# A hybrid decoder layer on one core: the state-space loop as small steps in one written order

## The chip, the core and the metric

One core of a Trainium2 chip runs the whole layer in one launch. Times are microseconds (us) on the device; the time of a kernel is the median of its runs. TensorE is called PE in the profile (PEld for its weight loads), VectorE DVE, ScalarE ACT, GpSimd POOL, and SyncE, which here only issues DMAs, SP. The profile comes from one further execution.

## What is computed

`x` is (1, 2048, 1024) float32. One layer:

```python
h = rmsnorm(x, pre_norm_g)
u_s, z_s, q, k, v, z_a, g_s, g_a = split(h @ w_in)              # 8192 columns
y_s = s5_branch(u_s, ...) * silu(z_s)
y_a = dilated_attention_branch(q, k, v) * silu(z_a)
merged = sigmoid(g_s) * (y_s @ w_branch_s) + sigmoid(g_a) * (y_a @ w_branch_a)
x = x + rmsnorm(merged @ w_out, post_norm_g)
```

The s5 branch has 32 groups of 16 channels, each with 64 complex states that decay along the sequence:

```python
lam_bar = exp(lam * dt);  b_bar = ((lam_bar - 1) / lam) * b
drive  = einsum('gpc,blgc->blgp', b_bar, ug)
states = associative_scan(a_r * a_l, a_r * b_l + b_r)(lam_bar, drive)
y = gelu(einsum('gcp,blgp->blgc', c, states).real + d_skip * u)
y = y * sigmoid(y @ w_glu + b_glu)
```

## The kernel before

`h` stays in SBUF as two float32r halves, `hhi` and `hlo`, and every product of it with a weight is made of three matmuls (high by high, high by low, low by high). A strip of `w_in` is 128 columns. A **bank** is one PSUM tile of 128x512 that PE fills: 24 matmuls of 512 columns for the strips of the gates (`proj`, L103) or 48 matmuls of 256 columns for the values (`values`, L118). Between the first projections and the attention there are 96 banks: 32 for the gate `g_s` (evicted by a tanh on ACT, L559), 16 for `z_s` (tanh on ACT, then one operation on DVE, `ze`, L571 and L572) and 48 for the values (a copy on ACT, `ve`, L121). Each evicted bank goes to DRAM by a DMA. `feed` (L577) hands the banks out one by one and loads the next pair of strips, four transfers `w_raw` and four splits `w_hi` (ACT, L43) and `w_lo` (DVE, L44), when a pair is used up.

In between the banks runs the state-space loop: 16 passes, each over a **pair** of groups. For a pair,

- `ssm_powers` makes the tables `q` and `out` on POOL;
- `ssm_setup` makes on PE a small kernel `pk` (L444) and a transpose `pt` (L458), evicts them (`kt` on DVE, L446; `inm` on ACT, L460), and writes `kt` to DRAM and reads it back as the Toeplitz matrix `toep`;
- `ssm_states` makes the rotations `rot_c` (POOL) and `rot_s` (DVE, L485 to L487), the drive `pd` on PE (L499, needs `inm`), its copy on ACT (L501), and then swaps halves of the partitions by two DMAs (L493, L494), rotates (POOL L506, DVE L505 and L507), scans (DVE L510), swaps again, and rotates back (POOL L516, DVE L515 and L519) into `st`;
- `ssm_outputs` makes `py` on PE (L529, L530, needs `st` and `toep`) and a gelu of it: a square on ACT (L537), two operations on DVE (L538, L539), a tanh on ACT (L540), one on DVE (L541), two DMAs.

What is in order: on PE the order is written by hand. `queued` (L594) ties each piece of PE work to the one before it, so in `run` a pass is `pd`, two banks, `py` of the pair before, a bank, `pk` and `pt` of the next pair, a bank. On the other engines and on the DMA queue of SP the order inside a pass is the scheduler's: the kernel is built with `schedule_with_timeline_sim=True`, and the scheduler sorts what is ready by its own estimate of time. Once built, each engine takes its instructions in the order in which they stand, and one that waits holds those behind it. After the loop come `glu`, the remaining banks, the attention (`unit`), its combination, the branch products and the output.

Of the kernel before, what the change touches and what calls it, by code (L numbers as in the profile page):

```python
# [34 lines left out]
class Builder:  # L35
    def __init__(self, tc, a):
        self.tc, self.nc, self.a = tc, tc.nc, a

# [54 lines left out]

    def proj(self, ps, w, s, chunk):
# [12 lines left out]
    def values(self, ev, psum, w, g, p):  # L107

        nc = self.nc
        hi, lo = w  # L110
        for r in range(0, 16, 2):
            ps = psum.tile([128, 2, 256], F32, tag="proj", name="pv")
            for o in range(2):
                rs = slice((r + o) * 128, (r + o) * 128 + 128)
                n = 0
                for k in range(8):
                    for st, m in ((self.hhi, hi), (self.hhi, lo), (self.hlo, hi)):
                        last = nc.tensor.matmul(ps[:, o], st[:, k, rs], m[:, k], start=n == 0, stop=n == 23)  # L118
                        n += 1
            e = ev.tile([128, 2, 256], F32, tag="ev", name="ve")  # L120
            nc.scalar.activation(e, ps, AF.Copy)  # L121
            cols = slice(256 * p, 256 * p + 256)
            if g == 0:
                dst = self.vd[0].rearrange("(i r) x -> i r x", r=16)[:, r : r + 2, cols]
            elif g == 1:
                m, c = divmod(r, 4)
                dst = self.vd[1].rearrange("(c i m) x -> m i c x", c=4, m=4)[m][:, c : c + 2, cols]
            else:
                dst = self.vd[2].rearrange("(r i) x -> i r x", r=16)[:, r : r + 2, cols]
            nc.sync.dma_start(dst, e)  # L130
            yield last
# [276 lines left out]
    def ssm_powers(self, g0, pool, tabd):  # L408

        nc = self.nc  # L410
        MUL, SUB = ALU.mult, ALU.subtract
        tab = pool.tile([128, 2, TAB], F32, name="tab", bufs=3)
        nc.sync.dma_start(tab, tabd[:, g0 : g0 + 2])
        sh = [128, 2, 16, 8]

        def power(which, n0):
            o = TABS[which][0] + n0
            return tab[:, :, o : o + 8].unsqueeze(2).to_broadcast(sh)

        def wide(which):  # L420
            o = TABS[which][0]
            return tab[:, :, o : o + 16].unsqueeze(3).to_broadcast(sh)

        g = nc.gpsimd
        t8 = pool.tile(sh, F32, name="t8")
        q = pool.tile(sh, F32, name="q", bufs=2)
        out = pool.tile(sh, F32, name="out", bufs=3)
        g.tensor_tensor(q, wide(6), power(4, 0), op=MUL)
        g.tensor_tensor(t8, wide(7), power(5, 0), op=MUL)
        g.tensor_tensor(q, q, t8, op=SUB)  # L430
        ot, t8t = (x.rearrange("p g c t -> p g (c t)").rearrange("p g (t c) -> p g c t", t=8) for x in (out, t8))
        g.tensor_tensor(ot, wide(8), power(4, 1), op=MUL)
        g.tensor_tensor(t8t, wide(9), power(5, 1), op=MUL)
        g.tensor_tensor(ot, ot, t8t, op=SUB)
        return tab, q, out

    def ssm_setup(self, g0, powers, pool, psum, kds):
        nc = self.nc
        tab, q, out = powers
        cs, dg = (tab[:, :, TABS[i][0] : TABS[i][0] + 16] for i in (8, 10))  # L440

        pk = psum.tile([128, 2, 16], F32, tag="s", name="pk")
        for j in range(2):
            nc.tensor.matmul(pk[:, j], q[:, j].rearrange("p c t -> p (c t)"), cs[:, j], start=True, stop=True)  # L444
        kt = pool.tile([128, 2, 16], F32, name="kt")
        nc.vector.tensor_tensor(kt, pk, dg, op=ALU.add)  # L446


        kd = kds[g0 // 2 % 2]
        toep = pool.tile([128, 2, 128], F32, name="toep", bufs=2)  # L450
        for j in range(2):
            nc.sync.dma_start(kd[j, :, 7:], kt[:, j])
            windows = bass.AP(tensor=kd.tensor, offset=kd[j].offset, ap=[[15 * 16, 16], [16, 8], [1, 128]])
            nc.sync.dma_start(toep[:, j], windows)

        pt = psum.tile([128, 2, 128], F32, tag="t", name="pt")
        for j in range(2):
            last = nc.tensor.transpose(pt[:, j], q[:, j].rearrange("p c t -> p (c t)"), self.ident)  # L458
        inm = pool.tile([128, 2, 128], F32, name="inm", bufs=2)
        nc.scalar.activation(inm, pt, AF.Copy)  # L460
        return last, (tab, inm, toep, out)

    def ssm_input(self, g0, pool):
        u = pool.tile([128, 2, 256], F32, name="u", bufs=2)
        ud = self.ud.rearrange("ch s k i -> (ch s) (k i)")
        self.nc.sync.dma_start(u, ud[g0 * 128 : g0 * 128 + 256].rearrange("(g p) x -> p g x", p=128))
        return u

    def ssm_states(self, g0, u, mats, pool, psum):

        nc = self.nc
        MUL, ADD, SUB = ALU.mult, ALU.add, ALU.subtract
        tab, inm, toep, out = mats

        sh = [128, 2, 16, 16]
        ca, sa = (tab[:, :, TABS[i][0] : TABS[i][0] + 16].unsqueeze(3).to_broadcast(sh) for i in (0, 1))
        cb, sb = (tab[:, :, TABS[i][0] : TABS[i][0] + 16].unsqueeze(2).to_broadcast(sh) for i in (2, 3))
        c, s = (pool.tile(sh, F32, name=n) for n in ("rot_c", "rot_s"))
        t = pool.tile(sh, F32, tag="sx", name="rot_t", bufs=SXB)
        w = pool.tile(sh, F32, tag="sx", name="rot_w", bufs=SXB)  # L480
        g = nc.gpsimd
        g.tensor_tensor(c, ca, cb, op=MUL)
        g.tensor_tensor(t, sa, sb, op=MUL)
        g.tensor_tensor(c, c, t, op=SUB)
        nc.vector.tensor_tensor(s, sa, cb, op=MUL)  # L485
        nc.vector.tensor_tensor(w, ca, sb, op=MUL)
        nc.vector.tensor_tensor(s, s, w, op=ADD)  # L487
        c = c.rearrange("p g a b -> p g (a b)")
        s = s.rearrange("p g a b -> p g (a b)")

        def swapped(x):
            y = pool.tile([128, 2, 256], F32, tag="sx", name="sx", bufs=SXB)
# [4 lines left out]
        pd = psum.tile([128, 2, 256], F32, tag="s", name="pd")  # L497
        for j in range(2):
# [79 lines left out]
    def feed(self, wp, items):  # L578
# [11 lines left out]
        while ready:  # L590
            yield from ready.pop(0)
            prepare()
# [582 lines left out]
```

## Time and profile before

| | |
|---|---|
| median of 3 runs | 2167.76 us (2166.22 to 2170.51) |
| the profiled execution's own time | 2165.64 us |
| its span, first to last instruction | 2163.8 us |
| PE busy | 2091.1 us, 97% of the span, 11668 matmuls |
| PEld, DVE, ACT, POOL busy | 83%, 42%, 27%, 18% |
| mean granted clock of TensorE | 0.988 |
| the loop, first `pd` (pair 0) to first `pd` of pair 15 | 231.40 to 665.34 us |

A timeline row gives start, duration, engine, line, operation, result and operands, and in square brackets how long the engine was idle before it and what ended that. Matmuls are pipelined, so a matmul's duration is longer than the distance to the next one's start; lengths of PE's work are therefore read from start to start.

### The profile page before, as it was taken

Reading aid. Unit: us, or ns where it says so; the run is one execution under the profiler, and the core shown is the slowest. Engines: PE = TensorE matmul, PEld = TensorE weight load, DVE = VectorE, ACT = ScalarE, POOL = GpSimd, SP = SyncE. Lnnn points to the kernel's source line nnn. Section 1 sums busy time; section 2 is a strip of 40 time slices with the busy share of each in tenths; the row PEclk is TensorE's granted clock in tenths of the full one; section 3 lists DMA queues with packets and bytes.
Section 4 is the critical chain, followed back from the end, with each engine's and each line's share of the span. In section 5 each row is a group of like instructions: output and inputs, shape, how many; then the busy total and the mean of one; then the engine's idle time right before and its main releaser. Section 6 shows DMA issues by size and latency. Waiting matters only on the chain.

```text
span 2163.8 us, 30793 instructions
## 1 busy us (share of the span) xinstructions
PE 2091.1 (97%) x11668; PEld 1799.8 (83%) x11668; DVE 915.1 (42%) x2261; ACT 587.6 (27%) x1327; POOL 388.1 (18%) x384
## 2 busy tenths in 40 slices
PE   8999999999989999999999999999899999999998
PEld 6788877798889997888888888888677878999987
DVE  6981345544443223423433442442512125544435
ACT  5421111111112323333433432443111124211211
POOL 0002344443331120000000000000555301111111
PEclk9999999999999999999999999999999999999999
DMA  7243233333333551111111111121666437343423
GB/s 251 90 149 131 84 102 99 92 96 109 106 93 113 167 153 45 43 60 58 59 50 59 60 50 59 54 64 54 185 214 188 144 117 224 104 147 107 122 78 98
DMA packets 208373, 231.50 MB, mean 107 GB/s; under 512 B 24864, under 2 KB 142944, under 8 KB 207968
## 3 DMA queue, kind: packets, MB, share of 16 engines
q1 hardware_dynamic: 208224, 229.54, 34.2%
q8 instruction: 91, 1.49, 0.3%
q14 instruction: 58, 0.48, 0.1%
HBM read 146.52 MB, written 74.56 MB: 102 GB/s over the span
## 4 chain that ended last, share of the span: by engine, by line
PE 67%; DMA 13%; DVE 9%; issue 3%; POOL 3%; SPq 2%; ACT 2%; DVEq 0%; POOLq 0%; ACTq 0%
PE proj L103 40%; PE br L937 7%; PE po L956 7%; DMA sx<-sx 3%; PE pv L118 3%; DMA cf<-fd 2%; PE s L762 2%; DMA w_raw<-in_wst_dram 2%; PE glu L634 1%; DMA kd<-kt 1%; PE nb L788 1%; DVE rot_s L485 1%; DMA raw<-in_wout_dram 1%; DVE sx L507 1%; POOL sx L506 1%
## 5 line engine op out<-in xcount | busy, mean ns | idle before, releaser
L103 PE MATMUL proj<-hhi,w_hi 128*128 128x512 f32 x1664 | 672.6, 405 | 27.9 <-DVE ze L572 12.5
L103 PE MATMUL proj<-hlo,w_hi 128*128 128x512 f32 x1664 | 667.4, 401 | 3.4 <-DVE hlo L44 2.7
L103 PE MATMUL proj<-hhi,w_lo 128*128 128x512 f32 x1664 | 666.2, 401 | 0.0
L103 PEld LDWEIGHTS proj<-hhi,w_hi 128*128 128x128 f32 x1664 | 315.6, 190 | 107.1 <-DVE ze L572 15.2
L103 PEld LDWEIGHTS proj<-hlo,w_hi 128*128 128x128 f32 x1664 | 315.6, 190 | 78.3 <-DVE hlo L50 3.5
L103 PEld LDWEIGHTS proj<-hhi,w_lo 128*128 128x128 f32 x1664 | 315.9, 190 | 71.8
L118 PE MATMUL pv<-w_hi,hhi 128*128 128x256 f32 x768 | 223.1, 291 | 4.5 <-ACT ve L121 2.7
L118 PE MATMUL pv<-w_lo,hhi 128*128 128x256 f32 x768 | 217.6, 283 | 0.0
L118 PE MATMUL pv<-w_hi,hlo 128*128 128x256 f32 x768 | 217.5, 283 | 0.0
L44 DVE TENSOR_TENSOR w_lo<-w_raw,w_hi 128x512 fp32r<-128x512 f32 (+1 forms) x130 | 93.1, 735 | 263.2 <-ACT w_hi L43 262.7
L118 PEld LDWEIGHTS pv<-w_hi,hhi 128*128 128x128 f32 x768 | 148.1, 193 | 6.2 <-ACT ve L121 3.3
L118 PEld LDWEIGHTS pv<-w_lo,hhi 128*128 128x128 f32 x768 | 148.0, 193 | 0.8
L118 PEld LDWEIGHTS pv<-w_hi,hlo 128*128 128x128 f32 x768 | 147.7, 192 | 0.0
L746 ACT ACTIVATE p<-p,nm 128x256 f32<-128x256 f32 (+1 forms) x192 | 89.5, 467 | 162.2 <-DVE nm L745 146.1
L740 DVE CUSTOM_DVE_ANT_0 p<-s,mask 128x256 f32<-128x256 f32 (+1 forms) x192 | 68.1, 375 | 144.9 <-PE t L821 69.6
L43 ACT ACTIVATE w_hi<-w_raw 128x512 fp32r<-128x512 f32 (+1 forms) x130 | 77.8, 620 | 180.3 <-DMA w_raw<-in_wst_dram 136.8
L940 POOL TENSOR_TENSOR gt<-gt 128x256 f32<-128x256 f32 x64 | 48.7, 764 | 388.7 <-DVE gt L939 226.2
L956 PE MATMUL po<-wout0h,mh 128*128 128x512 f32 x256 | 99.0, 392 | 2.1 <-ACT wout0h L43 2.1
L696 POOL CAST kh<-kh 128x128 fp32r<-128x128 f32 x12 | 4.0, 334 | 538.5 <-PE s L818 429.7
L956 PE MATMUL po<-wout0l,mh 128*128 128x512 f32 x256 | 99.9, 390 | 0.0
L956 PE MATMUL po<-wout0h,ml 128*128 128x512 f32 x256 | 99.5, 390 | 0.0
L559 ACT ACTIVATE ge<-proj 128x512 f32<-128x512 f32 x64 | 37.7, 592 | 180.0 <-PE proj L103 110.0
(249 smaller groups left out, 3369.8 us busy)
## 6 DMA issues: line engine op xcount, KB each, us to landing
w_raw<-in_wst_dram SPq DMA_DIRECT2D x126, 256.0 KB
vd<-ve SPq DMA_DIRECT2D x48, 256.0 KB
numd<-acc SPq DMA_DIRECT2D x48, 256.0 KB
cn<-numd SPq DMA_DIRECT2D x48, 256.0 KB
cf<-fd SPq DMA_DIRECT2D x48, 256.0 KB
xT<-in_xT_dram SPq DMA_DIRECT2D x32, 256.0 KB
gts<-ge SPq DMA_DIRECT2D x32, 256.0 KB
sx<-sx SPq DMA_DIRECT2D x64, 128.0 KB
```

The source lines that it names most:

```text
L43: nc.scalar.activation(hi, src, AF.Copy)
L44: nc.vector.tensor_tensor(lo, src, raw(hi), op=ALU.subtract)
L103: last = nc.tensor.matmul(ps, st[:, k, cs], m, start=n == 0, stop=n == 23)
L118: last = nc.tensor.matmul(ps[:, o], st[:, k, rs], m[:, k], start=n == 0, stop=n == 23)
L485: nc.vector.tensor_tensor(s, sa, cb, op=MUL)
L559: nc.scalar.activation(e, ps, AF.Tanh, scale=0.5)
L740: nc.vector.tensor_tensor_reduce(p[:, :n], scores, mask, scale=1.0, scalar=-3.0e38, op0=ALU.add, op1=ALU.max, accum_out=st[:, 0, blk : blk ...
L746: nc.scalar.activation(p[:, :n], p[:, :n], AF.Exp, scale=HEAD_SCALE, bias=nm, accum_out=st[:, 1, blk : blk + 1])
L762: nc.tensor.matmul(s[:, h], x[:, b], y[:, k0 : k0 + 2], start=n == 0, stop=n == 2)
L937: nc.tensor.matmul(ps, st[:, k, cs], m[:, i, k], start=n == 0, stop=n == 11)
L940: nc.gpsimd.tensor_tensor(gt[:, 0], gt[:, 0], gt[:, 1], op=ALU.add)
L956: nc.tensor.matmul(po[b, half], st[:, k, bs], m[:, k, hs], start=k == 0 and n == 0, stop=k == 7 and n == 2,)
```

## The change

The loop is cut into fifteen small functions per pair (`ssm_pair`), and a new function `ssm` writes all of them, for all engines, in one order. A bank is split into three callables: the product on PE, the eviction, the store. `program_order` then ties every instruction of the loop to the one written before it on the same engine (the DMA queue among them), without a semaphore, so that the scheduler can't reorder. Per pass there are four banks again, now placed as `pd`, a bank, `py` of the pair before, a bank, `pk` and `pt` of the next pair, two banks. The gelu of the pair before is written ahead of the rotation back; the rotation tables of the next pair behind its `kt`; of a pair of strips two parts of four are loaded and split per pass. Of the 96 banks 20 stand ahead of the first `pd` where 21 stood, and 12 are left for the time after the last `py` where 11 were. The arithmetic is the same.

```diff
+    @contextmanager
+    def program_order(self):
+        block = self.tc.nc.cur_bb
+        head = block.bb.instructions[-1]
+        yield
...
+        for ins in traced[first:]:
+            if ins.engine in last:
+                self.tc.add_manual_dep(
+                    ins, last[ins.engine],
+                    mybir.DependencyInfo(mybir.DependencyClass.NoSync, mybir.DependencyReason.DATA),
+                    reason="program_order",
+                )
+            last[ins.engine] = ins.name
...
+    def ssm(self, pool, psum, tabd, kds, strips):
+        pairs = [self.ssm_pair(2 * s, pool, psum, tabd, kds[s % 2]) for s in range(16)]
+        held = []
+        def do(s, *names):
+            if 0 <= s < 16:
+                for n in names:
+                    self.queued(pairs[s][n]) if n in ("matrices", "drive", "output") else pairs[s][n]()
+        def bank():
+            product, *rest = next(strips)
+            self.queued(product)
+            held.append(rest)
+        def leave():
+            if held:
+                for f in held.pop(0):
+                    f()
+        do(0, "table", "powers", "inputs")
+        do(1, "table", "powers")
+        do(0, "matrices", "input_matrix", "kernel", "rotation", "toeplitz")
+        self.products(strips, 2)
+        with self.program_order():
+            for s in range(16):
+                do(s, "drive")
+                leave()
+                do(s, "drive_out")
+                bank()
+                due = self.parts[:2]
+                del self.parts[:2]
+                for load, _ in due:
+                    load()
+                do(s + 2, "table")
+                do(s, "rotate", "scan")
+                leave()
+                do(s - 1, "output")
+                bank()
+                do(s - 1, "gelu")
+                do(s + 1, "inputs")
+                do(s, "rotate_back")
+                do(s + 1, "matrices")
+                leave()
+                bank()
+                do(s + 1, "input_matrix", "kernel")
+                for _, split in due:
+                    split()
+                do(s + 1, "rotation", "toeplitz")
+                do(s + 2, "powers")
+                leave()
+                bank()
+            leave()
+            do(15, "output", "gelu")
...
-                    products(18)
+                    self.products(strips, 16)
...
-                        for s in range(16):
-                            if s < 15:
-                                powers = self.ssm_powers(2 * s + 2, sw, tabd)
-                            state = queued("s", self.ssm_states, 2 * s, u, mats, sw, psum)
-                            products(2)
-                            if s:
-                                queued("o", self.ssm_outputs, *held, sw, psum)
-                            held = (2 * s, mats, *state)
-                            if s < 15:
-                                u = self.ssm_input(2 * s + 2, sw)
-                                products(1)
-                                mats = queued("m", self.ssm_setup, 2 * s + 2, powers, sw, psum, kds)
-                                products(1)
+                        self.ssm(sw, psum, tabd, kds, strips)
```

The names of `ssm_pair` say what they hold: `drive` is `pd`, `drive_out` its copy and the first swap, `rotate` and `scan` end with the second swap, `rotate_back` makes `st`, `output` is `py`, `matrices` is `pk` and `pt`, `input_matrix` is `inm`, `kernel` is `kt` with its two writes, `toeplitz` the two reads.

**DVE, one pass of the loop** (the pass that prepares pair 12). Before, from `rot_w` of the next pair to `kt`:

```order
L486 TENSOR_TENSOR rot_w<-tab 128x512
L515 TENSOR_TENSOR sx<-sx,rot_c 128x512
L519 TENSOR_TENSOR st<-sx 128x2x256
L485 TENSOR_TENSOR rot_s<-tab 128x512
L487 TENSOR_TENSOR rot_s<-rot_s,rot_w 128x512
L518 MEMSET st 128x2
L538 TENSOR_SCALAR gv<-gv 128x512
L539 TENSOR_TENSOR gv<-py,gv 128x512
L541 SCALAR_TENSOR_TENSOR gv<-gv,py 128x512
L446 TENSOR_TENSOR kt<-pk,tab 128x32
```

The same pass of the changed kernel, from the scan on:

```order
L575 SCALAR_TENSOR_TENSOR sx<-tab,sx 128x256 x2
L604 TENSOR_SCALAR gv<-gv 128x512
L605 TENSOR_TENSOR gv<-py,gv 128x512
L607 SCALAR_TENSOR_TENSOR gv<-gv,py 128x512
L584 MEMSET st 128x2
L585 TENSOR_TENSOR sx<-sx,rot_c 128x512
L586 TENSOR_TENSOR st<-sx 128x2x256
L512 TENSOR_TENSOR kt<-pk,tab 128x32
L65 TENSOR_TENSOR w_lo<-w_raw,w_hi 128x4x128 x2
L539 TENSOR_TENSOR rot_s<-tab 128x512
L540 TENSOR_TENSOR rot_w<-tab 128x512
L541 TENSOR_TENSOR rot_s<-rot_s,rot_w 128x512
```

The three gelu operations have moved from behind the rotation back and the rotation tables to a place right behind the scan.

**ACT, the same pass.** Before, from one copy of `pd` to the next:

```order
L501 ACTIVATE sx<-pd 128x2x2x128
L121 ACTIVATE ve<-pv 128x512 x2
L537 ACTIVATE gv<-py 128x512
L540 ACTIVATE gv<-gv 128x512
L121 ACTIVATE ve<-pv 128x512
L460 ACTIVATE inm<-pt 128x256
L121 ACTIVATE ve<-pv 128x512
L501 ACTIVATE sx<-pd 128x2x2x128
```

The changed kernel:

```order
L561 ACTIVATE sx<-pd 128x2x2x128
L165 ACTIVATE ve<-pv 128x512
L603 ACTIVATE gv<-py 128x512
L606 ACTIVATE gv<-gv 128x512
L165 ACTIVATE ve<-pv 128x512
L507 ACTIVATE inm<-pt 128x256
L64 ACTIVATE w_hi<-w_raw 128x4x128 x2
L165 ACTIVATE ve<-pv 128x512 x2
L561 ACTIVATE sx<-pd 128x2x2x128
```

`inm` still stands behind the tanh of the gelu, but two evictions of banks now lie between it and the next `pd`, where one lay.

## Rows read from the trace of the kernel before

**Rows 1.** The page, busy time of PE over the whole span.
```profile
PE 2091.1 (97%) x11668; PEld 1799.8 (83%) x11668; DVE 915.1 (42%) x2261; ACT 587.6 (27%) x1327; POOL 388.1 (18%) x384
```

**Rows 2.** Windows: stretch, length, busy time (and count) by engine, granted clock, DMA.
```profile
120.00:231.40 111.40, 111.40 (x482) 89.82 (x481) 43.81 (x206) 18.43 (x32) 18.75 (x22) 1.00 0.36 123
...
231.40:665.34 433.94, 400.83 (x2496) 360.07 (x2495) 212.99 (x252) 79.22 (x148) 178.14 (x153) 0.96 0.34 98
...
805.00:830.00 25.00, 22.47 (x120) 18.82 (x119) 7.05 (x21) 5.66 (x14) 4.50 (x8) 0.93 0.19 56
```

**Rows 3.** Waits of PE, 231 to 666: total, times, longest.
```profile
PE pd L499 <- ACT inm L460: 19.1, 8, 4.8
PE proj L103 <- DVE ze L572: 9.4, 6, 3.0
PE pv L118 <- DVE ze L572: 1.8, 1, 1.8
```

**Rows 4.** Timeline of PE, 249 to 275.
```profile
249.05 0.51 PE L444 MATMUL pk<-tab,q 128*128 128x16 f32 x4
...
249.59 0.47 PE L103 MATMUL proj<-hhi,w_hi 128*128 128x512 f32 x1
...
255.26 0.38 PE L499 MATMUL pd<-u,inm 128*128 128x256 f32 x1
...
267.32 0.38 PE L529 MATMUL py<-u,toep 128*128 128x256 f32 x1
...
274.68 0.29 PE L444 MATMUL pk<-tab,q 128*128 128x16 f32 x2
```

**Rows 5.** Timeline of PE, 566 to 579.
```profile
566.45 0.41 PE L458 MATMUL pt<-ident,q 128*128 128x128 f32 x2
...
576.42 1.13 PE L499 MATMUL pd<-u,inm 128*128 128x256 f32 x4 [3.94 <-ACT inm L460]
```

**Rows 6.** Timeline of ACT, 566 to 580.
```profile
574.97 0.63 ACT L540 ACTIVATE gv<-gv 128x512 f32<-128x512 f32 x1 [13.69 <-DVE gv L539]
...
575.99 0.38 ACT L460 ACTIVATE inm<-pt 128x256 f32<-128x256 f32 x1
...
577.58 0.63 ACT L501 ACTIVATE sx<-pd 128x512 f32<-128x512 f32 x1 [0.73 <-PE pd L499]
```

**Rows 7.** Timeline of DVE, 239 to 577.
```profile
239.65 1.27 DVE L510 TENSOR_TENSOR_SCAN sx<-tab,sx 128x256 f32<-128x256 f32 x2
...
560.92 1.39 DVE L507 TENSOR_TENSOR sx<-sx 128x512 f32<-128x512 f32 x1
562.35 1.28 DVE L510 TENSOR_TENSOR_SCAN sx<-tab,sx 128x256 f32<-128x256 f32 x2
...
568.58 1.55 DVE L519 TENSOR_TENSOR st<-sx 128x512 f32<-128x512 f32 x1 [1.19 <-POOL sx L516]
570.06 1.77 DVE L485 TENSOR_TENSOR rot_s<-tab 128x512 f32<-128x512 f32 x1
571.87 1.02 DVE L487 TENSOR_TENSOR rot_s<-rot_s,rot_w 128x512 f32<-128x512 f32 x1
572.82 1.39 DVE L538 TENSOR_SCALAR gv<-gv 128x512 f32<-128x512 f32 x1
...
574.25 0.69 DVE L539 TENSOR_TENSOR gv<-py,gv 128x512 f32<-128x512 f32 x1
...
576.24 0.18 DVE L446 TENSOR_TENSOR kt<-pk,tab 128x32 f32<-128x32 f32 x1
```

**Rows 8.** Timeline of POOL, the rotation back of two pairs.
```profile
245.48 1.80 POOL L516 TENSOR_TENSOR sx<-sx,rot_s 128x512 f32<-128x512 f32 x1 [6.41 <-DMA sx<-sx]
...
566.72 1.83 POOL L516 TENSOR_TENSOR sx<-sx,rot_s 128x512 f32<-128x512 f32 x1 [4.96 <-DMA sx<-sx]
```

**Rows 9.** Groups by line, 231 to 666: count, busy, mean ns, idle before and what ended it.
```profile
L44 DVE TENSOR_TENSOR w_lo<-w_raw,w_hi 128x512 fp32r<-128x512 f32 x30 | 22.3, 765 | 49.2 <-ACT w_hi L43 49.2
...
L540 ACT ACTIVATE gv<-gv 128x512 f32<-128x512 f32 x14 | 8.8, 632 | 152.3 <-DVE gv L539 152.3
```

More of the change, by code (lines that the diff above doesn't have):

```diff
@@ L1 @@
+from contextlib import contextmanager
 import numpy as np
@@ L37, in __init__ @@
         self.tc, self.nc, self.a = tc, tc.nc, a
+    @contextmanager
[3 more added lines that the diff above has]
+        yield
+        assert self.tc.nc.cur_bb is block
+        traced = list(block.bb.instructions)
+        first = next(k for k in reversed(range(len(traced))) if traced[k] is head) + 1
+        last = {}
+        for ins in traced[first:]:
[6 more added lines that the diff above has]
+            last[ins.engine] = ins.name
     def split(self, hi, lo, src, scale=None):
@@ L110, in values @@
         hi, lo = w
-        for r in range(0, 16, 2):
[L112 to L131, printed above, removed]
+        cols = slice(256 * p, 256 * p + 256)
@@ L437, in ssm_setup @@
[L437 to L461, printed above, removed]
@@ new lines, in matrices, with input_matrix @@
+        def matrices():
+            pk = m["pk"] = psum.tile([128, 2, 16], F32, tag="s", name="pk")
+            for j in range(2):
+                nc.tensor.matmul(pk[:, j], flat(m["q"], j), cols(8)[:, j], start=True, stop=True)
+            pt = m["pt"] = psum.tile([128, 2, 128], F32, tag="t", name="pt")
+            for j in range(2):
+                last = nc.tensor.transpose(pt[:, j], flat(m["q"], j), self.ident)
+            return last
+        def input_matrix():
+            m["inm"] = pool.tile([128, 2, 128], F32, name="inm", bufs=2)
+            nc.scalar.activation(m["inm"], m["pt"], AF.Copy)
@@ L495, in swapped @@
             return y
-        pd = psum.tile([128, 2, 256], F32, tag="s", name="pd")
-        for j in range(2):
-            last = nc.tensor.matmul(pd[:, j], inm[:, j], u[:, j], start=True, stop=True)
-        d = pool.tile([128, 2, 256], F32, tag="sx", name="sx", bufs=SXB)
-        nc.scalar.activation(
-            d.rearrange("p g (i k) -> p g k i", k=2), pd.rearrange("p g (k i) -> p g k i", k=2), AF.Copy
-        )
-        e = swapped(d)
-        nc.vector.tensor_tensor(d, d, c, op=MUL)
@@ new lines, in drive, with drive_out @@
+        def drive():
+            pd = m["pd"] = psum.tile([128, 2, 256], F32, tag="s", name="pd")
+            for j in range(2):
+                last = nc.tensor.matmul(pd[:, j], m["inm"][:, j], m["u"][:, j], start=True, stop=True)
+            return last
+        def drive_out():
+            m["d"] = wide_tile()
+            nc.scalar.activation(
+                m["d"].rearrange("p g (i k) -> p g k i", k=2), m["pd"].rearrange("p g (k i) -> p g k i", k=2), AF.Copy
+            )
+            m["e"] = swapped(m["d"])
@@ new lines, in ssm_pair @@
+        return {f.__name__: f for f in (
+            table, powers, matrices, input_matrix, kernel, toeplitz, inputs, rotation, drive, drive_out,
+            rotate, scan, rotate_back, output, gelu,
+        )}
+    def ssm(self, pool, psum, tabd, kds, strips):
[47 more added lines that the diff above has]
+            do(15, "output", "gelu")
@@ L592, in feed, with weights_due, products @@
             prepare()
+    def weights_due(self):
+        for load, split in self.parts:
+            load()
+            split()
+        self.parts.clear()
+    def products(self, strips, n=None):
+        for i, (product, evict, store) in enumerate(strips):
+            self.weights_due()
+            self.queued(product)
+            evict()
+            store()
+            if i + 1 == n:
+                return
     def queued(self, emit):
```

289 lines of the change are left out of this document (161 added, 128 removed).

## The prediction

> **What bounds the kernel now.** I read the page first: PE is busy 97% of the span [rows 1], so at first sight nearly nothing is left. Then I cut the span into windows, because that share is a mean. From 120 to 231.4 us PE has no idle time and a granted clock of 1.00; in the loop, from the first `pd` of pair 0 to that of pair 15, it is busy 400.83 of 433.94 us, so 33.1 us idle, at a clock of 0.96 [rows 2]. PE is the engine that sets the end, so time that the loop gives back moves everything behind it forward.
>
> Busy time is not the whole loss, so I measured the loop from start to start on PE. A stretch in which PE waits for nothing gives the length of each piece [rows 4]: `pk` and `pt` 249.59 - 249.05 = 0.54, one bank 255.26 - 249.59 = 5.67, `pd` and two banks 267.32 - 255.26 = 12.06, `py` and a bank 274.68 - 267.32 = 7.36. A whole pass without waits is 12.06 + 7.36 + 0.54 + 5.67 = **25.63 us**. The first pass, which has no `py`, runs unhindered from 231.40 (where that window of rows 2 begins) to 255.26, 23.86 us. Fifteen passes would take 23.86 + 14 x 25.63 = 382.7 us; they took 433.94. **The loop loses 51.3 us.** A cross-check from other rows: 33.1 us idle, and a mean clock of 0.96 costs 4% of 433.94, 17.4 us; together 50.5. A mean of 0.96 mixes the two levels, 1.2 and 2.4 GHz; so some 17 us are not waits, and they stand where waits are, since without waits the clock is 1.00.
>
> By the Trainium skill (Perfetto Trace Analysis, Identifying the Most-Contended Engine) matmul busy time is a poor measure of headroom, and the busy share of weight loads should be taken. By that share, 360.07 of 433.94 us [rows 2], the sum would be 73.9 us to regain; by matmul busy time 33.1. The trace agrees with the warning and not with the substitute: weight loads are busy 81% of the stretch from 120 to 231.4 us, where PE never stops, so I give the time by that share, 2165.64 - 73.9 = 2091.7, no chance.
>
> **What PE waits for.** The table of waits names `inm`, 19.1 us in 8 waits, and `ze`, 9.4 + 1.8 us [rows 3]. One pass shows how a small eviction comes late. `pt` begins at 566.45; its eviction `inm` begins 9.54 us later, and `pd` starts after 3.94 us of idle PE [rows 5, 6]. ACT was not busy: the instruction ahead of `inm` is the tanh of another pair's gelu, and it waited 13.69 us for DVE. DVE meanwhile did the rotation back, the rotation tables of the next pair and only then the two gelu operations, at 572.82 and 574.25 [rows 7]. That tanh waits 152.3 us in its 14 turns in the loop [rows 9]. So the loop runs round a chain that has no need to be one: `pd`, swap, scan, swap, rotation back, tables, gelu, tanh, `inm`, next `pd`.
>
> **The change part by part.** I put one pass of the written order on a clock that starts with `pd`, with durations from the old rows.
>
> PE: `pd` and a bank end at 12.06 - 5.67 = 6.4, `py` and a bank at 13.8, `pk` and `pt` at 14.3, two banks at 25.6. The pieces and their count are those of before, so nothing is added on PE.
>
> The first chain: the copy of `pd` ends at 1.79 (577.58 + 0.63 - 576.42) [rows 5, 6]. A swap, two issues and the landing, takes from the end of a scan to the rotation back on POOL 3.09 us in one pair (563.63 to 566.72) and 4.56 in another (240.92 to 245.48) [rows 7, 8]; I keep both as bounds. The product on POOL is 1.83 [rows 8], the sum 1.39, the scan 1.28 [rows 7]: the scan ends at 9.4 to 10.9. The gelu stands next on DVE (1.39 + 0.69), then the tanh on ACT (0.63): it ends at **12.1 to 13.6**, before the second bank ends at 13.8. So the eviction of that bank and `inm` follow `pt` at once, near 15.3, and `pd` wants `inm` at 25.63: about 10 us of cover, where before one bank lay between. The 19.1 us and the clock behind them go.
>
> The rest of DVE's line: second swap (3.09 to 4.56), POOL 1.83, `st` 1.55: 15.9 to 18.8. `st` is wanted by `py` in the next pass, near 32. Then `kt` 0.18, two `w_lo` at 0.77 [rows 9], three operations of the rotation at 1.77 or less, and for the sixteen banks with a `ze` one more operation (0.69, the row of the same shape) [rows 7]: 0.18 + 1.53 + 1.77 + 1.77 + 1.02 + 0.69 = 7.0 us, ending at 22.9 to **25.8**. That `ze` frees the PSUM buffer that the first bank of the next pass takes at 25.63 + 0.68 = 26.3 (0.68 is 12.06 less two banks at 5.69). So it fits, in the worst case by half a microsecond, in four passes of sixteen; elsewhere ACT alone frees the bank. The 11.2 us of `ze` waits go.
>
> POOL: 178.14 / 15 = 11.9 us of work per pass [rows 2], the rotation back ending by 17.3 and 8.3 us of tables behind it, by 25.6; its next product is wanted at 25.63 + 4.9. The tables have a whole further pass. SP: each pass issues what it issued before; the first swap now stands behind the store of one finished bank, the second behind two weight loads and a table whose buffers the last pass has freed; the Toeplitz matrix, which waits for `kt` to land, holds only the stores of two banks behind it. If these come some us late, a bank's buffer is still free a pass earlier than needed. Weights come two parts per pass, and a pair of strips lasts two passes: costed at nothing, hidden by those passes; without the cover each would show one transfer.
>
> Outside the loop: one bank moves from ahead of it to behind it, at no cost. Between 805 and 830 us, where the attention begins, PE is idle 2.53 us and the clock is 0.93, 1.75 more [rows 2]. The order there changes as a by-product (the first scores stand a bank later). Between no gain and 4.3 us I take half, 2.2.
>
> Sum, against the profiled execution's own 2165.64: 2165.64 - 51.3 - 2.2 = 2112.1 us. The median of the runs, 2167.76, stands 2.1 above that execution, so for a median I forecast **2114.2 us**.
>
> **The rivals.** *Part of it stays.* If only idle time comes back and the low clock stays, or if the `ze` waits (11.2 us and their share of the clock, 5.9) stay behind DVE's line, the gain is 33 to 34: 2165.64 - 33.1 - 2.2 + 2.1 = 2132.4. For it: the half microsecond of cover above. Against it: four passes only, and the clock is 1.00 for over 110 us where nothing waits. Chance 0.08.
>
> *Slower: DVE and ACT held by the swaps.* In the written order the gelu stands behind the first swap, and the eviction of the second bank behind its tanh. With a swap of w us the tanh ends at 9.0 + w and that eviction 0.6 later; the fourth bank needs the buffer at 13.8 + 0.54 + 5.67 = 20.0. From w = 10.4 on, each further us costs PE one per pass. The gain is used up and 0.2% lost when (51.3 + 4.3) / 16 = 3.5 us are lost per pass, from w = 13.9; at 15 us the time would be near 2165.6 + 16 x 4.6 - 51.3 = 2188. The scheduler could put something else into such a gap, a written order can't. Against it: 3.09 and 4.56 measured, with the DMA engines 34% busy [rows 2] and no more bytes than before. Chance 0.04.
>
> *No change.* The order rows show that the instructions do move; it would take a wait that isn't in these rows, such as another buffer, that makes a pass 28.9 us again (433.94 / 15). Time 2167. Chance 0.03.
>
> **How the numbers follow.** The forecast's own cases (loop without waits) reach from 2108 (all 4.3 us at the attention, the glu stage a little better, the median close to the profile) to 2122 (half a microsecond per pass left); chance 0.85. The range goes on to the first rival: 2106 to 2134. About 0.2%, 4.3 us, is what a measurement of this kernel can tell from no change (three runs spread over 4.3). Faster 0.93, same 0.03, slower 0.04.
>
> **What would show it.** Right: in the window of the loop PE idle near 0, a clock of 1.00, `pd` to `pd` 25.6 us in every pass; `inm` less than 2 us behind `pt`; the tanh's wait for DVE cut from about 11 us a turn to 1 or 2; the loop near 383 us. Wrong: PE waits for `ze` or for an eviction in the passes with `z_s` banks (first rival), swaps over 10 us with ACT waiting in front of an eviction (second), or passes still near 29 us with a new name in the table of waits (third). A gain well over 51 us would mean that stages outside the loop moved too.

## The result and the profile after

The changed kernel takes 2113.06 us (median of 6 runs, 2109.73 to 2116.26), the kernel before in the same sitting 2168.34 (6 runs, 2165.22 to 2170.51). The ratio is 0.975, 95% interval 0.9737 to 0.9762. The forecast was 2114.2. The profiled execution's own time is 2111.86 us, its span 2110.1.

The page and three windows of the changed kernel; in a window: stretch, length, busy time (and count) of PE, PEld, DVE, ACT and POOL, granted clock, DMA share, GB/s. They answer to [rows 1, 2]. The third window reaches from the last `glu` matmul to the 21st `s` of the attention; the row below it is that stretch of the kernel before.

```profile
PE 2073.4 (98%) x11668; PEld 1788.3 (85%) x11668; DVE 901.1 (43%) x2261; ACT 593.5 (28%) x1327; POOL 403.8 (19%) x384
```

```profile
120.00:227.37 107.37, 107.37 (x465) 86.55 (x464) 45.18 (x212) 18.80 (x33) 14.18 (x16) 1.00 0.34 120
227.37:610.39 383.02, 383.02 (x2471) 347.36 (x2470) 196.09 (x251) 82.61 (x146) 199.92 (x159) 1.00 0.39 114
754.57:781.65 27.08, 27.08 (x131) 21.98 (x130) 6.70 (x19) 6.37 (x16) 3.00 (x6) 1.00 0.13 38
```

```profile
812.29:836.21 23.92, 21.39 (x100) 17.18 (x99) 7.05 (x20) 6.38 (x17) 3.02 (x6) 0.93 0.12 36
```

The second window is the loop, from the first `pd` to that of pair 15. It takes 383.02 us where it took 433.94; PE is never idle in it and the granted clock is 1.00. The busy share of PE over the whole span has moved by one point, from 97 to 98%: the page's first line would not have told where 55 us were.

The waits of PE over the whole span of the changed kernel (total, times, longest), which answer to [rows 3]:

```profile
PE proj L137 <- ACT ge L688: 8.6, 4, 5.1
PE proj L137 <- ACT hhi L70: 6.4, 2, 5.4
PE proj L137 <- DVE ze L690: 3.2, 1, 3.2
```

`pd` no longer waits for `inm`. What is left lies outside the loop, above all `hhi` at the start of the kernel, `ge` and `ze` in the combination behind the attention.

One pass of the changed kernel, the one whose `pd` starts at 379.44, on ACT, then on DVE; they answer to [rows 6, 7].

```profile
390.03 0.63 ACT L606 ACTIVATE gv<-gv 128x512 f32<-128x512 f32 x1 [1.56 <-DVE gv L605]
393.46 0.60 ACT L688 ACTIVATE ze<-proj 128x512 f32<-128x512 f32 x1 [2.80 <-PE proj L137]
394.08 0.38 ACT L507 ACTIVATE inm<-pt 128x256 f32<-128x256 f32 x1
394.36 1.14 ACT L64 ACTIVATE w_hi<-w_raw 128x512 fp32r<-128x512 f32 x2
```

```profile
386.28 0.69 DVE L569 TENSOR_TENSOR sx<-sx 128x512 f32<-128x512 f32 x1 [1.18 <-POOL sx L567]
387.01 1.27 DVE L575 TENSOR_TENSOR_SCAN sx<-tab,sx 128x256 f32<-128x256 f32 x2
...
388.78 0.42 DVE L604 TENSOR_SCALAR gv<-gv 128x512 f32<-128x512 f32 x1
389.30 0.69 DVE L605 TENSOR_TENSOR gv<-py,gv 128x512 f32<-128x512 f32 x1
...
393.28 1.55 DVE L586 TENSOR_TENSOR st<-sx 128x512 f32<-128x512 f32 x1 [1.18 <-POOL sx L583]
...
397.93 1.14 DVE L539 TENSOR_TENSOR rot_s<-tab 128x512 f32<-128x512 f32 x1
398.99 1.13 DVE L540 TENSOR_TENSOR rot_w<-tab 128x512 f32<-128x512 f32 x1
```

The gelu's two operations stand ahead of the rotation back; the tanh starts 10.6 us after `pd` (390.03 - 379.44), the eviction of the second bank and `inm` follow when PE has finished, at 14.0 and 14.6. Every pass but the first, which has no `py`, is 25.63 to 25.70 us long.

The groups of ACT in the loop that changed most, of the changed kernel and then one of the kernel before that the prediction did not read (count, busy, mean ns, idle before and what ended it); the first answers to the last of [rows 9]:

```profile
L606 ACT ACTIVATE gv<-gv 128x512 f32<-128x512 f32 x14 | 8.8, 632 | 20.8 <-DVE gv L605 20.8
...
L64 ACT ACTIVATE w_hi<-w_raw 128x512 fp32r<-128x512 f32 x28 | 16.0, 622 | 0.0
```

```profile
L43 ACT ACTIVATE w_hi<-w_raw 128x512 fp32r<-128x512 f32 x30 | 17.9, 624 | 54.4 <-DMA w_raw<-in_wst_dram 49.7 <-PE proj L103 4.7
```

The tanh's idle time fell from 152.3 to 20.8 us, as foreseen. But ACT of the kernel before also stood 49.7 us in front of weight splits for their transfers, and now it stands there not at all. In seven of fourteen passes (the odd ones from 1 to 13) two of these splits stand on ACT ahead of the copy of `pd`. This is the pass that the prediction took as its example; its `pd` starts at 545.95. ACT of the kernel before:

```profile
551.79 0.63 ACT L43 ACTIVATE w_hi<-w_raw 128x512 fp32r<-128x512 f32 x1 [6.63 <-DMA w_raw<-in_wst_dram]
552.33 0.58 ACT L121 ACTIVATE ve<-pv 128x512 f32<-128x512 f32 x1
553.32 0.63 ACT L43 ACTIVATE w_hi<-w_raw 128x512 fp32r<-128x512 f32 x1 [0.41 <-DMA w_raw<-in_wst_dram]
553.85 0.63 ACT L501 ACTIVATE sx<-pd 128x512 f32<-128x512 f32 x1
```

The copy begins 7.9 us after `pd`, in the changed kernel 1.1. In the seven passes it came 4.2 to 9.7 us after `pd`, and these lost 33.5 of the 51.3 us, the seven even ones 17.7 (each pass's length less 25.63). The odd passes' part is larger than that: passes 8, 10, 12 and 14 run at a clock of 0.90 to 0.94, behind the waits for `inm` of 2.8 to 4.8 us that end the passes ahead of them, and this is about half of the 17.7. So there were two suspects for one gain: the place of the gelu (theory P, the prediction's), and the weight splits ahead of the copy (theory W). A third is that any fixed order helps (theory O).

### The profile page after: what moved, and what is told of

It is laid out like the page before. It is cut to its first block, busy times and chain, and to the rows that moved or that the text cites. A ratio compares the mean times of both kernels' runs of the same rounds, so it can differ in the third digit from the quotient of the medians.

```text
span 2110.1 us, 30798 instructions
## 1 busy us (share of the span) xinstructions
PE 2073.4 (98%) x11668; PEld 1788.3 (85%) x11668; DVE 901.1 (43%) x2261; ACT 593.5 (28%) x1327; POOL 403.8 (19%) x384
## 4 chain that ended last, share of the span: by engine, by line
PE 87%; DMA 7%; DVE 2%; ACT 1%; POOL 1%; issue 1%; SPq 0%; DVEq 0%; ACTq 0%; POOLq 0%
PE proj L137 48%; PE pv L159 12%; PE br L1084 8%; PE po L1103 7%; DMA cf<-fd 2%; PE s L909 2%; PE glu L781 2%; PE nb L935 1%; PE na L935 1%; DMA cn<-numd 1%; PE nc L973 1%; PE py L593 1%; POOL cn L1025 1%; PE s L965 1%; PE pd L556 1%
## 5 line engine op out<-in xcount | busy, mean ns | idle before, releaser
L159 PE MATMUL pv<-w_hi,hhi 128*128 128x256 f32 x768 | 218.8, 285 | 0.0
L65 DVE TENSOR_TENSOR w_lo<-w_raw,w_hi 128x512 fp32r<-128x512 f32 (+1 forms) x130 | 111.5, 881 | 207.7 <-ACT w_hi L64 207.1
```

Source lines behind the costliest of these rows:

```text
L65: nc.vector.tensor_tensor(lo, src, raw(hi), op=ALU.subtract)
```

## The experiments

The loop of every kernel, from the first `pd` to that of pair 15, with the idle time of PE and the granted clock in it, and the median of the whole kernel. Loop, idle time and clock are those of the one profiled execution of each kernel. The ratio is to runs of the kernel before in the same sitting.

| kernel | loop us | PE idle | clock | median us | ratio, 95% |
|---|---|---|---|---|---|
| before | 433.94 | 33.1 | 0.96 | 2168.34 | |
| changed | 383.02 | 0 | 1.00 | 2113.06 | 0.975 (0.9737 to 0.9762) |
| changed, gelu late | 439.94 | 37.6 | 0.96 | 2170.89 | 1.0019 (1.0006 to 1.0033) |
| changed, gelu behind `inm` | 393.61 | 7.5 | 1.00 | 2122.57 | 0.9791 (0.9771 to 0.9811) |
| changed, splits first | 416.53 | 21.1 | 0.97 | 2152.33 | 0.9929 (0.9908 to 0.9951) |
| the same, weights in time | 386.28 | 2.1 | 1.00 | 2115.42 | 0.9766 (0.9752 to 0.9781) |
| changed, gelu late and splits first | 509.08 | 91.2 | 0.90 | 2242.85 | 1.035 (1.0323 to 1.0376) |
| the same, weights in time | 517.11 | 102.0 | 0.89 | 2253.13 | 1.0399 (1.0382 to 1.0415) |
| before, splits behind the copy | 413.29 | 21.0 | 0.98 | 2147.24 | 0.9919 (0.9902 to 0.9936) |
| before, gelu ahead | 391.83 | 4.3 | 0.99 | 2121.57 | 0.979 (0.9774 to 0.9807) |
| before, both | 383.92 | 0.5 | 1.00 | 2118.57 | 0.9769 (0.9747 to 0.9791) |
| changed, `pt` a bank later | 382.99 | 0 | 1.00 | 2112.62 | 0.9745 (0.9724 to 0.9767) |
| changed, long swap | 384.27 | 0.8 | 1.00 | 2115.63 | 0.976 (0.9735 to 0.9785) |
| changed, more buffers behind the loop | | | | 2113.72 | 0.9746 (0.9723 to 0.9768) |

### The changed kernel with the gelu late

```diff
-                do(s - 1, "gelu")
                 do(s + 1, "inputs")
                 do(s, "rotate_back")
+                do(s + 1, "rotation")
+                do(s - 1, "gelu")
                 do(s + 1, "matrices")
...
-                do(s + 1, "rotation", "toeplitz")
+                do(s + 1, "toeplitz")
```

> The written order kept, but the gelu's place in the old order restored: on DVE behind the rotation back and the next pair's rotation tables, on ACT its tanh ahead of the second bank's eviction and of inm. Theory P (the place of the gelu ahead of an eviction is what costs): in the changed kernel the rotation back ends 15.2 us after pd; three table operations of 1.1 and the gelu's two give a tanh that ends near 20.5 to 21.0, the eviction behind it near 21.1 to 21.6 (0.7 later still in the four passes of z_s), and the fourth bank wants that buffer at 19.96. So PE waits 1.1 to 2.4 us for the eviction in every pass: 18 to 35 us in 15 passes with a little clock, time 2131 to 2148, pd to pd 26.8 to 28. Theory W (the weight splits ahead of the copy of pd are what cost) and theory O (it is pinning any order at all that pays): 2113.

Measured: 2170.89 us, the whole gain gone with the gelu put back behind the rotation back and the next tables (which move up with it, ahead of it, as they stood before); the rest keeps the written order. The direction is theory P's, and theories W and O are out as the whole story; the size is 58 us where 18 to 35 was expected. DVE, ACT and PE of one pass (its `pd` at 277.40):

```profile
293.13 1.56 DVE L539 TENSOR_TENSOR rot_s<-tab 128x512 f32<-128x512 f32 x1
294.62 1.77 DVE L540 TENSOR_TENSOR rot_w<-tab 128x512 f32<-128x512 f32 x1
296.42 1.02 DVE L541 TENSOR_TENSOR rot_s<-rot_s,rot_w 128x512 f32<-128x512 f32 x1
297.37 0.86 DVE L604 TENSOR_SCALAR gv<-gv 128x512 f32<-128x512 f32 x1
```

```profile
299.07 0.63 ACT L606 ACTIVATE gv<-gv 128x512 f32<-128x512 f32 x1 [12.64 <-DVE gv L605]
299.60 0.58 ACT L689 ACTIVATE ge<-proj 128x512 f32<-128x512 f32 x1
300.08 0.38 ACT L507 ACTIVATE inm<-pt 128x256 f32<-128x256 f32 x1
```

```profile
297.20 0.40 PE L137 MATMUL proj<-hhi,w_lo 128*128 128x512 f32 x1
300.23 0.50 PE L137 MATMUL proj<-hhi,w_hi 128*128 128x512 f32 x1 [2.63 <-ACT ge L689]
...
301.03 0.62 PE L137 MATMUL proj<-hhi,w_hi 128*128 128x512 f32 x1
301.45 0.63 PE L137 MATMUL proj<-hlo,w_hi 128*128 128x512 f32 x1
```

PE's fourth bank starts when the eviction behind the tanh is done. The expectation erred twice. The table operations took 1.56 and 1.77 us, not 1.1: here they run beside POOL operations of 1.53 and 1.62 us, in the changed kernel beside ones of 1.1 (last section). And I allowed "a little clock": after the wait of 2.63 us the matmuls follow one another every 0.42 to 0.43 us instead of 0.23, the lower of the two levels, 1.2 GHz, from 301.03 to 304.44. Over the loop the clock is 0.96, which costs 4% of 439.94, 17.6 us, on top of 37.6 idle; the kernel before lost 33.1 and 17.4.

### The gelu later still, but ahead of nothing

```diff
-                do(s - 1, "gelu")
...
                 do(s + 1, "rotation", "toeplitz")
+                do(s - 1, "gelu")
                 do(s + 2, "powers")
```

> The written order kept, the gelu later still: behind the rotation back, inm, kt, the weight splits and the next tables, so that its tanh stands ahead of no eviction that is wanted soon (on ACT only the third bank's, wanted at 26.3). Theory P: the gelu is late on DVE by 10 us, its tanh ends near 21, and nobody waits: 2111 to 2116. If lateness of the gelu itself (its py buffer, the store, DVE's line) is what costs: as the run with the late gelu or worse, 2131 to 2160.

Measured: 2122.57, 9.5 us above the changed kernel; 6.6 above what was expected at most. The tanh begins at 23 us after `pd` and later, in some passes only in the next pass, and the third bank's eviction, which stands behind it, is then late by up to 1.8 us. ACT and PE, where the next `pd` starts at 458.91:

```profile
460.51 0.63 ACT L606 ACTIVATE gv<-gv 128x512 f32<-128x512 f32 x1 [10.70 <-DVE gv L605]
461.05 1.07 ACT L165 ACTIVATE ve<-pv 128x512 f32<-128x512 f32 x2
```

```profile
461.68 0.39 PE L159 MATMUL pv<-w_hi,hhi 128*128 128x256 f32 x1 [1.75 <-ACT ve L165]
```

The loss is a sixth of the 58 us although the gelu is later: what costs is mostly not the gelu's lateness but how urgent the eviction is that stands behind its tanh.

### The weight splits ahead of the copy of `pd`, alone and with the late gelu

```diff
                 leave()
-                do(s, "drive_out")
                 bank()
...
                     load()
+                for _, split in due:
+                    split()
+                do(s, "drive_out")
...
-                for _, split in due:
-                    split()
```

This is the edit of the second form. In the first, the loads and splits stood ahead of `bank()` as well.

> The written order kept, but the two weight parts of a pass are loaded and split ahead of the copy of pd, as seven passes of the old trace have it. On ACT the copy then waits for the transfer: about 3 us from issue to landing, and 5 to 6 us after pd instead of 1.1. Theory P: the scan ends at 13 to 14, the tanh near 15.5, the second bank's eviction near 16, wanted at 19.96; the end of DVE's line moves from 21.7 to about 26, wanted at 26.3 and only in the four passes of z_s: no loss, 2112 to 2118. Theory W: the 5 us come back as a loss in every pass, 2113 + 15 x 3 to 5 = 2158 to 2188.

Measured: 2152.33, outside of what theory P allowed, but for a fault of the edit. `bank()` is what asks for the next strips; with the loads ahead of it the parts came a pass later than in the changed kernel, and PE waited for them:

```profile
PE pv L159 <- ACT w_hi L64: 21.7, 5, 4.6
```

Four passes of some 33 us carry this; passes without it and without `z_s` (8, 10, 12, 14) are 25.65 us long with the copy 6 us after `pd`. So I ran it again with the parts in time.

> As the run with the splits ahead of the copy, but with the weight parts taken behind the pass's first bank product, so that they aren't a pass later than in the changed kernel (that cost four passes 7 us each of PE waiting for w_hi, which has nothing to do with the question). The copy of pd is again 4.5 to 6 us late. Theory P: the passes without z_s keep 25.65 us, as passes 8, 10 and 12 of that run did; the four with z_s lose 0.5 to 2 each: time 2114 to 2122. Theory W: 3 to 5 us in every pass, 2158 to 2188.

Measured: 2115.42, loop 386.28. The copy is 5.6 to 6.7 us after `pd` in passes 1 to 14, and passes without `z_s` keep 25.64 to 25.72 us; the four with it (3 to 6) lose 0.5 to 1.1. With the gelu in its new place the late copy is nearly free, and theory W falls as an explanation by itself. The two displacements together:

> Both of these in the written order: the weight splits ahead of the copy of pd, and the gelu late with its tanh ahead of an eviction. Theory P with the copy as a link of the same chain: the tanh ends 5 us later than with the late gelu alone, near 25.5 to 26, the eviction near 26.5 where 19.96 is wanted: 6 to 7.5 us in each of 15 or 16 passes, 2205 to 2235, with lost clock up to 2250; slower than the kernel before. If the two add and do not multiply (each costs what it costs alone): the sum of the two other runs' losses, 2131 to 2155.

> Both displacements, with the weight parts in time. Theory P (one chain, of which the copy is a link and the tanh's eviction the end): the late gelu alone stops PE for 2 to 2.6 us a pass; with the copy 5 us later it is 7 to 7.5, and a pass takes 22.3 + 5 + 5.7 and 1.5 to 2.5 of low clock, 34.5 to 35.5: 15 passes of it make the loop some 131 us longer than the changed kernel's, 2235 to 2255. If the two only add: the loss of the late gelu (57) and that of the splits alone (1 to 9), 2171 to 2180.

Measured: 2242.85 with the parts late, 2253.13 with the parts in time; the first is mixed with the weight waits of the faulty edit (22.2 us), the second is clean. ACT of the second in the pass whose `pd` starts at 427.50:

```profile
453.63 0.63 ACT L606 ACTIVATE gv<-gv 128x512 f32<-128x512 f32 x1 [17.11 <-DVE gv L605]
454.17 0.58 ACT L689 ACTIVATE ze<-proj 128x512 f32<-128x512 f32 x1
```

The tanh starts at 26.1 us after `pd`, the passes are 34.1 to 37.8 us long. In the medians the late gelu alone costs 58 us and the late copy alone 2, and together they cost 140; in the loop it is 56.9, 3.3 and 134.1. They are links of one chain: a delay early in it is free as long as the chain has slack, and counts in full once the chain sets the pass.

### One pin at a time in the kernel before

Here the scheduler keeps its freedom and instructions are tied behind another one on their engine. For the splits, the second strip's loads and splits are written behind the drive, and on ACT issued behind the copy:

```diff
+                            with self.tc.issue_after(self.copied.ins):
+                                for f in self.later:
+                                    f()
```

> The kernel before, order still the scheduler's, with one thing pinned: the second strip's two weight splits stand on ACT behind the copy of pd (in the old trace seven passes have them ahead, and the copy comes 4 to 10 us late). Theory P: these seven passes become like the other seven, which lose 2.5 us each because the gelu stands late: of the 33.5 us that they lose now some 16 remain, time near 2150 (2145 to 2158). Theory W (the splits are the root): they come to the floor of 25.63, and the even passes improve too: 2118 to 2135. If the splits were only hidden time: 2167.

Measured: 2147.24, as theory P had it: 19 us of the gain. The total fits better than its parts: of the 30.6 us that the loop still loses against 382.7 the odd passes have 19.2 and the even ones 11.4, where 16 and 17.7 were expected. For the gelu, rotation back and tables are issued behind its second operation on DVE:

```diff
+        with self.tc.issue_after(self.gv.ins) if self.gv else nullcontext():
             nc.vector.tensor_tensor(s, sa, cb, op=MUL)
...
+                            with self.tc.issue_after(self.gv.ins) if s else nullcontext():
+                                state[2]()
```

(`state[2]` is the rotation back, now a function of its own.)

> The kernel before, order still the scheduler's, with one thing pinned: the gelu's two DVE operations stand ahead of the rotation back and of the next tables. The splits stay where they were, ahead of the copy of pd in every second pass. Theory P: with the tanh at 15 to 16 us after pd instead of 24 to 31, inm is ready near 21 and wanted at 25.63, and the splits' transfers start earlier as well, because the buffers they wait for are freed behind that tanh: nearly all comes back, 2115 to 2130. Theory W: the seven passes with splits keep their 4.8 us each, 2147 to 2155.

Measured: 2121.57: 44 of the 55 us come back by this one pin. In the pass whose `pd` starts at 466.45, ACT:

```profile
473.82 0.63 ACT L46 ACTIVATE w_hi<-w_raw 128x512 fp32r<-128x512 f32 x1 [1.44 <-DMA w_raw<-in_wst_dram]
474.36 0.62 ACT L505 ACTIVATE sx<-pd 128x512 f32<-128x512 f32 x1
...
483.96 0.63 ACT L547 ACTIVATE gv<-gv 128x512 f32<-128x512 f32 x1 [2.87 <-DVE gv L546]
486.14 0.60 ACT L124 ACTIVATE ve<-pv 128x512 f32<-128x512 f32 x1 [1.55 <-PE pv L121]
```

The copy of `pd` still comes 7.9 us after it, behind the splits, the tanh comes at 17.5, and the next eviction waits for PE again, not the other way round; the pass is 25.66 us long. One part of my expectation was wrong: the splits' transfers did not come earlier, the copy stays 4.1 to 9.9 us behind `pd` in the odd passes; why these transfers land late stays open. It just no longer matters much: passes 3 and 5 still take 29.7 and 29.5 us, 11 and 13 lose half a microsecond, the others nothing. The profiled execution, 2128.71 us, is the slowest of the four (2117.40 to 2128.71), so the loop of a median run is probably shorter than the table's 391.83.

> The kernel before, order the scheduler's, with both pins: the gelu's two DVE operations ahead of the rotation back and the tables, and the second strip's splits behind the copy of pd. Theory P: what the gelu pin alone left (4 us in each of passes 3 and 5, under 1 in passes 11 and 13) goes too, and the loop stands at PE's floor: 2111 to 2118, the changed kernel's time, without its written order for all engines. Theory O (the rest of the changed order brings something of its own): 2121 as with the gelu pin alone.

Measured: 2118.57, half a microsecond above theory P's range, the loop 383.92. So two pins give the loop what the fully written order gives it. The remaining 5 us to the changed kernel lie outside: at the first `pd` of pair 15 this kernel is 49.70 us ahead of the kernel before, the changed one 49.26 (54.95, less the moved bank of 5.69). But here PE still waits 2.1 us at the first scores of the attention and the clock falls to 0.93 there, as in the kernel before; in the changed kernel neither happens.

### Two tests of cover

```diff
-                do(s + 1, "matrices")
                 leave()
                 bank()
-                do(s + 1, "input_matrix", "kernel")
...
                 do(s + 2, "powers")
+                do(s + 1, "matrices")
                 leave()
                 bank()
+                do(s + 1, "input_matrix", "kernel", "toeplitz")
```

> The changed kernel with pk, pt, inm and kt one bank later, so that one bank (5.67 us) lies between pt and the pd that needs inm, as in the kernel before, not two. Theory P: inm follows pt by 0.4 us, one bank is cover enough; kt and the Toeplitz transfers come some 6 us later and are wanted a pass later: 2111 to 2118. Rival: the changed kernel gains by the second bank of cover; then pd waits for inm again, 2 us or more in a pass, 2145 or more.

Measured: 2112.62, loop 382.99. With `pk`, `pt`, `inm` and `kt` moved one bank later, `inm` begins at 20.2 us and `pd` waits for nothing. The second bank of cover, which the change also brings and the prediction counted as 10 us of room, is not what pays.

In the next run each swap goes through DRAM.

```diff
-            y = wide_tile()
-            nc.sync.dma_start(y[0:64], x[64:128])
-            nc.sync.dma_start(y[64:128], x[0:64])
+            h = self.scr.tile([128, 2, 256], F32, name="hop")
+            nc.sync.dma_start(h, x)
+            y = wide_tile()
+            nc.sync.dma_start(y[0:64], h[64:128])
+            nc.sync.dma_start(y[64:128], h[0:64])
```

> The changed kernel with every swap of the halves sent through DRAM (one transfer out, two back), so that a swap takes some 5.5 to 6.5 us instead of 3.2: 5 to 6 us more on the chain from pd to the rotation back. Theory P: with the loop no longer closed through the tanh, only the end of DVE's line moves, from 21.7 to 27 or 28; wanted at 26.3 in the four passes of z_s alone: 0.5 to 1.5 us in each of these, 2113 to 2121. If the chain still closes over the pass: 5 us and their clock in each of 15 passes, 2190 or more.

Measured: 2115.63, loop 384.27. `st` ends 18.5 to 21.0 us after `pd` instead of 15.1 to 17.2, some 3 to 4 us for both swaps, less than the 5 to 6 aimed at. One pass, number 4, is 26.76 us long; the others are at most 25.77. The chain has room and no longer closes on itself.

### A try at what is left

> The changed kernel, loop untouched, with five eviction buffers for the gate strips of the combine stage instead of two. There PE still stands 11.7 us in five waits for an eviction, and those evictions wait on ACT up to 7.6 us for the store that frees their buffer, which stands on SP behind loads of the combination. Theory (the same kind of wait as in the loop, through another in-order queue): the five waits mostly go, 6 to 15 us, 2098 to 2107. Rival (the strips there are held by DVE or by their weights anyway): 2109 to 2114.

```diff
+class Turns:
+    def __init__(self, *pools):
+        self.pools, self.n = pools, 0
+    def tile(self, *args, **kw):
+        self.n += 1
+        return self.pools[(self.n - 1) % len(self.pools)].tile(*args, **kw)
...
+                    evg = Turns(ev, ev, more, more, more)
```

Measured: 2113.72, no gain. ACT of this kernel in the combine stage:

```profile
1503.44 0.58 ACT L697 ACTIVATE ge<-proj 128x512 f32<-128x512 f32 x1
1515.67 0.63 ACT L73 ACTIVATE w_hi<-w_raw 128x512 fp32r<-128x512 f32 x1 [11.65 <-DMA w_raw<-in_wst_dram]
1516.20 0.58 ACT L697 ACTIVATE ge<-proj 128x512 f32<-128x512 f32 x1
...
1528.39 0.60 ACT L697 ACTIVATE ge<-proj 128x512 f32<-128x512 f32 x1 [5.01 <-PE proj L146]
```

The evictions no longer wait for the store of a buffer; the last row waits for PE, as it should. But PE's five waits there add up to 15.8 us, where they were 11.8. The eviction at 1516.20, on which PE then stands 3.05 us, has a weight split ahead of it that waited 11.65 us for its transfer. It is the pattern of the loop before, at another place, and I had named the wrong link, or only one of two. Pinning those splits behind the evictions was not tried, so what it would bring stays open.

## Why the prediction was right

- **The loop.** 383.02 us were measured where 382.7 were predicted. The sum was made from PE's starts in a stretch without waits, and each pass behind the first takes what it said: 25.63 to 25.70 for 25.63.
- **The clock.** It returned with the idle time: 0.96 to 1.00 here, and back to 0.96 with the late gelu, with nearly the same idle time. That a third of the loss is not idle time was right: 50.92 came where PE was idle for 33.11. That the cross-check hit so well (17.4 from a mean clock of 0.96) is in part the rounding. In the trace's records of the granted clock the loss at the lower level adds up to 15.4 us, 1.5 of it while PE stood idle anyway, so some 4 us are neither idle time nor clock and stay open. Nor does the cross-check hold everywhere. With both displacements (weights in time) the same sum over the clock gives 56 us, but the loop is only 32 longer than its idle time explains, because 25 of the 56 lie inside the waits.
- **The cause.** That the gelu's place on DVE, through the tanh ahead of evictions on ACT, closes a chain over the pass is shown from both sides: put back, it costs the changed kernel 58 us; moved alone, it gives the kernel before 44.
- **A link that was missed.** The chain was given as `pd`, swap, scan, swap, rotation back, tables, gelu, tanh, `inm`. In half of the passes it also ran through the weight splits ahead of the copy of `pd`, and the rows of the example begin too late in its pass to show it. Of the gain 19 us can be had at this link alone. "Weights come two parts per pass: costed at nothing" holds for the changed kernel, whose splits begin 14.9 to 15.0 us after `pd` in passes 1 to 14 and wait for no transfer, but that the change takes them out of the chain was not in my account. The sum did not depend on it, being made from PE alone.
- **The clock of one pass.** The scan ends 8.6 to 10.6 us after `pd` (9.4 to 10.9 said), the tanh at 10.9 to 13.0 (12.1 to 13.6), `inm` starts at 14.6 (near 15.3). The swap came out like the shorter bound, 3.3 us from the end of the copy (381.18) to POOL's product (384.45). DVE's line ends at 24.3 at the latest, so the `z_s` passes had 2 us and more to spare, not half of one: the operations that I took at 1.39 took 0.69 and 0.42.
- **POOL** works 199.92 us in the loop where the prediction kept the 178.14 of before. It hid behind the pass all the same.
- **Outside the loop.** At the attention's first scores PE no longer stands. From the last `glu` matmul to the 21st `s` the kernel before took 23.92 us at a clock of 0.93, the changed one 27.08 at 1.00 with 32 matmuls `proj` more (98 and 66), which at 0.24 us from start to start are 7.7: for the same work 4.5 us less, so the upper bound of 4.3 and not the 2.2 taken. Some of it went elsewhere: before the loop PE is 4.03 us early with a bank of 5.69 fewer, and the lead falls from 55.30 us in the attention (958.18 and 902.88, the first `nc`) to 53.45 at the branch products (1791.59 and 1738.14). Over the span 53.7 us are gained, of which 50.9 in the loop. That the 2.8 outside come near 2.2 is luck: they are gains and losses of which the prediction knew one.
- **The rivals.** No `z_s` wait is left in the loop; the swaps, through which it could have become slower, cost the loop 1.3 us in the run that made them longer; and the instructions did move.
- The share of weight loads, which the Trainium skill (Perfetto Trace Analysis, Identifying the Most-Contended Engine) recommends for judging headroom, would have given 73.9 us. Without any wait it is now 347.36 of 383.02 us, 91%, so 100% was never there to be reached; 50.9 came.

## What to carry to other kernels

Where a loop's passes are longer than the work of the engine that sets the end, follow one whole pass, from its first instruction and over every in-order queue, and ask which late instruction an urgent eviction merely stands behind. A few order pins at such places can bring what a fully written order brings, as two did here; and a delay measured alone says little about its price while another delay keeps the chain closed, or open. Idle time on PE has a second price, most of it in the clock behind it, here about half as much again (17.8 beside 33.1 us before, 19.3 beside 37.6 with the late gelu), and less where the waits are long (32 beside 102).

## What the runs showed that was not expected

The same DVE operation can take two to three times as long when POOL works beside it. `d + e` of 128x512 takes 0.69 us in the changed kernel, POOL idle, and 1.39 in the kernel before [rows 7], where POOL's table operation of L483 ran from 560.23 for 1.53; the first operation of the gelu takes 0.42 instead of 1.39. The second one, which reads `py` from PSUM, takes 0.69 either way. In the run with the late gelu `rot_s` begins on DVE at 293.13 and ends at 294.69, with POOL at:

```profile
292.62 1.53 POOL L537 TENSOR_TENSOR rot_t<-tab 128x512 f32<-128x512 f32 x1
294.22 1.62 POOL L538 TENSOR_TENSOR rot_c<-rot_c,rot_t 128x512 f32<-128x512 f32 x1
```

DVE's operation ends 0.54 us after POOL's (294.15), the next one, at 296.39, 0.55 us after POOL's next (295.84): as if most of its work came only then. The Trainium skill says so (SBUF — State Buffer, Who interferes with whom): a DVE instruction with two SBUF inputs and a GpSimd instruction that reads SBUF contend, and the later one is blocked until the other is done. These rows agree. The first operation of the gelu has one input, so that sentence doesn't cover it, and no run here shows why it is slowed. A written order thus also sets which tables run side by side on the two engines: the changed kernel has POOL idle during the sum, the scan and the gelu.
